# A chain of its own for the queries of an attention layer, and the softmax's division on another engine

## Chip, cores and metric

The kernel runs on one core of one Trainium2 chip. The metric is the device time of one execution in microseconds, as the median of several runs. TensorE (PE in the rows) multiplies matrices, VectorE (DVE) and ScalarE (ACT) work on rows of 128 partitions, GpSimd (POOL) and SyncE (SP) issue most of the DMAs. Each engine works through its own queue in order, and an instruction waits at the head of its queue until its inputs are there and its output's buffer is free.

## What is computed

A two-layer decoder over 528 positions (16 learned ones and 512 of the input), width 1024. Each layer is half a SwiGLU, a mixer, and half a SwiGLU. The mixer of layer 0 is a recurrent one (RWKV-7), which the change does not touch. The mixer of layer 1 is an attention over selected keys; this is what matters here:

```python
q, k, v, qi, ki, wi = jnp.split(h @ w_in, ATT_SPLITS, axis=-1)
q = partial_rope(rms_norm(q.reshape(B, T, 16, 64), q_g), cos, sin)
k = partial_rope(rms_norm(k.reshape(B, T, 4, 64), k_g), cos, sin)
# an indexer scores all keys for each query; the 128 best causal ones count
logits = jnp.einsum("bqgrd,bqkgd->bqgrk", qg, kg).astype(jnp.float32) * scale
logits = jnp.where(valid[:, :, None, None, :], logits, -jnp.inf)
p = jax.nn.softmax(logits, axis=-1).astype(v.dtype)
o = jnp.einsum("bqgrk,bqkgd->bqgrd", p, vg)
```

There are 16 query heads in 4 groups of 4; a group shares one key and one value head.

## The kernel before

Matrix products that need float32 accuracy are made of three faster ones: each operand is split into a rounded part (`_hi`) and the rest (`_lo`). Weights stream from DRAM in units of 1024 columns (`wraw`), ScalarE rounds them (`whi`), VectorE takes the rest (`wlo`).

The positions are worked in two ranges, A (16 to 272) and B (272 to 528). The program has main streams, one after another: feed-forward halves (`ffn`), projections (`idx`, `kvq`), the attention's output projection (`ao`). They use PSUM banks `acc`. Beside them run chains: generators that issue a piece of work and yield what the next piece needs. `run` (L726) takes the main stream piece by piece and, by a list of prices (`Clock`), puts in a piece of a chain when its inputs should be there by the time TensorE gets to it, or when the main stream would have to wait. Chains are held back when VectorE or ScalarE would fall too far behind TensorE (`full`: 1500 ns for the stages kvqA and f10b, 3000 by default and for f11a). `drain` (L747) issues all that is left of the chains, with no main stream beside it. So the order on each engine is fixed when the program is built.

The attention of range A is laid beside the streams kvqA and f10b (the feed-forward half of the other range) and must be over before `ao` of range A; a `drain` stands there. Range B is laid beside kvqB and f11a, with a `drain` before `ao` of range B.

`attend(i, XO)` (L1621) does 128 queries, i from 1 to 4; `Wd` = 16 + 128 i keys, so 144, 272, 400 and 528. A range is two of them (`attend_range`, L1734): 1 and 2, then 3 and 4. Its parts, by heads or groups:

- `turn_q(g)` (L1630): the queries of a group are copied twice side by side (`qsd`, ScalarE), turned by TensorE (4 transposes into a bank `bg`), scaled and rounded into `qs` (ScalarE), and the rest is taken (VectorE). `qs` has 2 buffers, `qsd` 1. The helper is `stacked`.
- `logits(c)` (L1633), a step c of 0 to 7 with two heads: the score matmuls (`bg<-kT,qs`; 4, or 8 in two halves for 528 keys), on VectorE a custom instruction that adds the selection's bias and takes the row minimum (`pr<-bg,bias`, `mn`), on ScalarE the exponential with its row sum (`pr<-pr,mn`, `sm`).
- `divide(hh)` (L1659): the sum's reciprocal and the product, both on VectorE.
- `turn(hh)` (L1664): the probabilities are transposed by TensorE (`bg<-ident,pr`) and copied to `pt` by ScalarE. `pr` has 4 buffers.
- `values(g)` (L1678): the products with V for a group (`ry<-pt,V`); after an odd group ScalarE and VectorE split the result into `xa_hi`, `xa_lo` (or `xb_`).

There are 3 banks `bg` for all chains and one bank `ry`. The loop in `attend` goes over c from 0 to 8: `values` of the group that is complete, `logits(c)`, `turn_q` of the next group after an odd c, and then `divide` and `turn` of the heads of step c - 1.

Of the kernel before, what the change touches and what calls it, by code (L numbers as in the profile page):

```python
# [13 lines left out]
AF = mybir.ActivationFunctionType  # L14
OP = mybir.AluOpType
# [11 lines left out]
QA = (16, 272)  # L27
QB = (272, 528)
# [11 lines left out]
QG, OKA = 152, 154  # L40
# [393 lines left out]
def trunk(ctx, tc, wall, units, h0, vec, cstd, gqk, out, stop=None, gap=0.0, share=400.0, slack=200.0, fulls={}):  # L434
    clock = Clock()
    nc = Core(tc.nc, clock)
# [50 lines left out]
    def col(c):  # L487
        return vecs[:, c:c + 1]
# [4 lines left out]
    def bbank(tag="bg"):  # L493
        return psum.tile([128, 512], F32, name=tag, bufs={"bg": 3, "ry": 1}[tag])
# [213 lines left out]
    def beside(*gens):  # L708
        chains.extend(Chain(g) for g in gens)
        return chains[-len(gens)]  # L710
# [712 lines left out]
    kT = at.tile([128, 4, T], F32R, name="kT")  # L1423
# [6 lines left out]
    qx = {}  # L1430
    have = set()
# [84 lines left out]
    def segments(Wd):  # L1516
        return [(0, Wd)] if Wd <= 512 else [(0, Wd // 2), (Wd // 2, Wd)]
# [103 lines left out]
    def attend(i, XO):  # L1621


        Wd = 16 + 128 * i
        nb = i + 1
        b = bias[i - 1]
        sm = at.tile([128, 16], F32, name="sm", bufs=1)
        pr, pt, po, qs = {}, {}, {}, {}

        def turn_q(g):  # L1630
            qs[g] = yield from stacked("qs", 2, qx[i, g // 2][:, 256 * (g % 2):256 * (g % 2) + 256], col(QG))

        def logits(c):  # L1633

            g = c // 2
            mn = {}
            for o in (0, 1):
                pr[2 * c + o] = at.tile([128, T], F32, name="pr", bufs=4)
                mn[o] = at.tile([128, 2], F32, name="mn", bufs=4)
            sg = segments(Wd)  # L1640
            for j, (s0, s1) in enumerate(sg):
                yield "bg", qs[g], kT[:, g, s0:s1]
                ps = [bbank()[:, :s1 - s0] for _ in range(2)]
                for o in (0, 1):
                    for k in (0, 1):
                        nc.tensor.matmul(ps[o], qs[g][:, k, 2 * (c % 2) + o], kT[:, g, s0:s1],
                                         start=k == 0, stop=k == 1)
                for o in (0, 1):
                    nc.vector.tensor_tensor_reduce(out=pr[2 * c + o][:, s0:s1], in0=ps[o], in1=b[:, s0:s1],
                                                   scale=1.0, scalar=3e38, op0=OP.add, op1=OP.min,  # L1650
                                                   accum_out=mn[o][:, j:j + 1])
            for o in (0, 1):
                lg = pr[2 * c + o]
                if len(sg) == 2:
                    nc.vector.tensor_tensor(mn[o][:, 0:1], mn[o][:, 0:1], mn[o][:, 1:2], op=OP.min)
                nc.scalar.activation(lg[:, :Wd], lg[:, :Wd], AF.Exp, bias=mn[o][:, 0:1], scale=-1.0,
                                     accum_out=sm[:, 2 * c + o:2 * c + o + 1])

        def divide(hh):  # L1659
            r = sm[:, hh:hh + 1]  # L1660
            nc.vector.reciprocal(r, r)
            nc.vector.tensor_scalar(pr[hh][:, :Wd], pr[hh][:, :Wd], r, None, op0=OP.mult)

        def turn(hh):  # L1664
            if hh % 4 == 0:
                pt[hh // 4] = at.tile([128, 5, 4, 128], F32, name="pt", bufs=1)
            to = pt[hh // 4][:, :, hh % 2 * 2 + hh % 4 // 2]
            for k0 in range(0, nb, 4):
                ks = range(k0, min(k0 + 4, nb))
                yield "bg", pr[hh][:, :Wd]  # L1670
                p = bbank()
                pv = p.rearrange("p (m t) -> p m t", t=128)
                for kb in ks:
                    t0 = TOK[kb][0]
                    nc.tensor.transpose(pv[:, kb - k0], pr[hh][:, t0:t0 + 128], ident)
                nc.scalar.activation(to[:, k0:k0 + len(ks)], pv[:, :len(ks)], AF.Copy)

        def values(g):  # L1678

            q, c0 = g // 2, 256 * (g % 2)  # L1680
            yield "ry" if g % 2 == 0 else po[q][:, c0:c0 + 256], pt[g]
            if g % 2 == 0:
                po[q] = bbank("ry")
            for kb in range(nb):
                for o in (0, 1):
                    nc.tensor.matmul(po[q][64 * o:64 * o + 64, c0:c0 + 256], V[:, kb, 64 * g:64 * g + 64],
                                     pt[g][:, kb, 2 * o:2 * o + 2].rearrange("p h t -> p (h t)"),
                                     start=kb == 0, stop=kb == nb - 1)
            if g % 2:
                pv = po[q].rearrange("p (m t) -> p m t", t=128)  # L1690
                s = slice(TOK[i][0] - XO.t0, TOK[i][1] - XO.t0)
                hi, lo = XO.hi[:, 4 * q:4 * q + 4, s], XO.lo[:, 4 * q:4 * q + 4, s]
                nc.scalar.activation(hi, pv, AF.Copy)
                nc.vector.tensor_sub(lo, pv, hi.bitcast(F32))

        yield from turn_q(0)
        for c in range(9):
            if c % 2 and c > 1:
                yield from values(c // 2 - 1)
            if c < 8:  # L1700
                yield from logits(c)
            if c in (1, 3, 5):
                yield from turn_q((c + 1) // 2)
            if c:
                for hh in (2 * c - 2, 2 * c - 1):
                    divide(hh)
                for hh in (2 * c - 2, 2 * c - 1):
                    yield from turn(hh)
        yield from values(3)
        yield 0  # L1710
# [13 lines left out]
    def chain(*gs):  # L1724
        for g in gs:
            yield from g
# [4 lines left out]

    XO = {}

    def attend_range(q, i, name):  # L1734
        while ("q", i + 1) not in have or i - 1 not in bias:
            yield None
        XO[q] = Split(xq, DT, q, name)
        yield from attend(i, XO[q])
        while i not in bias:
            yield None  # L1740
        yield from attend(i + 1, XO[q])
# [3 lines left out]
    def heads_chain():  # L1745

        for _ in range(3):
            while not hs:
                yield None
            yield from hs[0]  # L1750
            hs.pop(0)
# [5 lines left out]
    QI = tiles_of((1, 2, 0), "xb_hi")  # L1757
    run(early(idx(XS["xa"], QI, (0, 1, 2)), norms[3], B))
    beside(heads_chain(), chain(*(idx_heads(i, QI) for i in (0, 1, 2)), select(0), select(1)))
    beside(attend_range(QA, 1, "xa"))  # L1760
    run(early(kvq(XS["xa"], (0, 1, 2)), norms[3], B, X=x_of(B, "xb"), start=40), "kvqA")
    have.add(QA)
    run(ffn(1, 0, B, XS["xb"], hid_of(B), norms[4]), "f10b")
# [2 lines left out]
    QI = tiles_of((3, 4), "xa_hi")  # L1766
    run(early(idx(XS["xb"], QI, (3, 4)), norms[5], QA))
    beside(heads_chain(), chain(idx_heads(3, QI), idx_heads(4, QI), select(2), select(3)))
    beside(attend_range(QB, 3, "xb"))
    run(early(kvq(XS["xb"], (3, 4)), norms[5], QA, X=x_of(QA, "xa"), start=40), "kvqB")  # L1770
    have.add(QB)
    run(ffn(1, 1, QA, XS["xa"], hid_of(QA), None, done=write), "f11a")
# [63 lines left out]
```

## Time and profile before

| | us |
|---|---|
| median of 3 timed runs | 2361.96 (2358.84 to 2363.72) |
| the profiled run | 2355.84 |
| its span in the trace | 2354.1 |
| TensorE busy | 2264.1 |
| VectorE busy | 1704.5 |
| ScalarE busy | 1263.8 |

A span is shorter than the run's time by what lies before the first and behind the last instruction. A busy share is a mean over stages with different limits, so it is read by stretches; the attention of range A starts near 1608 and that of range B near 1955 us from the span's start. In the rows a matmul's duration includes a tail that the next one overlaps; PEclk is TensorE's granted clock, 1.00 for the upper level (2.4 GHz) and 0.50 for the lower.

### The profile page before, as it was taken

To read this page: it belongs to the slowest core of one execution; us is meant where nothing else is said; L and a number is where in the kernel's file an instruction comes from. 1 tells how busy PE (TensorE), PEld (TensorE's weight loads), DVE (VectorE), ACT (ScalarE), POOL (GpSimd) and SP (SyncE) were. 2 spreads that over 40 slices of the span, in tenths; PEclk is the share of its full clock that TensorE was granted. 3 is DMA by queue.
4 is the path that set the end of the run, shared out by engine and by line. 5 is a ranking of instruction groups with operands and counts; after the bars stand their busy time and mean duration, and the time that the engine had idled before them with its cause. 6 is when DMAs were issued, how large, how long until landed. Compare 5 with 4: busy or idle time off the path is not lost.

```text
span 2354.1 us, 49396 instructions
## 1 busy us (share of the span) xinstructions
PE 2264.1 (96%) x20106; PEld 2177.3 (92%) x20106; DVE 1704.5 (72%) x3283; ACT 1263.8 (54%) x2135; POOL 175.5 (7%) x226
## 2 busy tenths in 40 slices
PE   8998899999989999999999999999988999999999
PEld 8998889999889999999999999899977899988999
DVE  7667888856897975677566565689755898766665
ACT  5443665465548535655444444556664646775543
POOL 0001521010043111000000000000000000000000
PEclk9999999999999999999999999999989999999999
DMA  6553334632434444245554555455532453434554
GB/s 231 180 172 123 119 126 162 205 86 83 144 118 157 156 161 147 74 135 171 174 178 171 180 187 177 148 171 174 167 117 79 147 179 129 159 117 135 185 183 144
DMA packets 101555, 355.98 MB, mean 151 GB/s; under 512 B 11552, under 2 KB 15728, under 8 KB 101328
## 3 DMA queue, kind: packets, MB, share of 16 engines
q1 hardware_dynamic: 99120, 347.91, 44.5%
q0 software_dynamic: 2208, 4.92, 0.8%
q8 instruction: 158, 2.59, 0.4%
q14 instruction: 69, 0.57, 0.1%
HBM read 348.51 MB, written 4.28 MB: 150 GB/s over the span
## 4 chain that ended last, share of the span: by engine, by line
PE 79%; DVE 13%; ACT 4%; issue 2%; DMA 1%; POOL 1%; SPq 0%; DVEq 0%; ACTq 0%; POOLq 0%
PE acc L341 68%; PE bg L341 8%; DVE wlo L341 4%; PE ry L341 4%; DVE tb L341 2%; ACT whi L341 1%; DVE pr L341 1%; DMA wraw<-wall 1%; ACT pr L341 1%; DVE ynat L341 0%; DVE h L341 0%; DVE st L341 0%; DVE m L341 0%; DVE bu L341 0%; DVE rel L341 0%
## 5 line engine op out<-in xcount | busy, mean ns | idle before, releaser
L341 DVE TENSOR_TENSOR wlo<-wraw,whi 128x1024 fp32r<-128x1024 f32 (+1 forms) x658 | 810.4, 1235 | 167.4 <-ACT whi L341 166.6
L341 ACT ACTIVATE whi<-wraw 128x1024 fp32r<-128x1024 f32 (+1 forms) x658 | 688.3, 1051 | 437.6 <-PE acc L341 265.8
L341 PE MATMUL acc<-hid_hi,whi 128*128 128x256 f32 (+1 forms) x1408 | 407.4, 289 | 3.4 <-DVE h L341 2.2
L341 PE MATMUL acc<-hid_lo,whi 128*128 128x256 f32 (+1 forms) x1408 | 399.1, 283 | 0.8 <-DVE hid_lo L341 0.8
L341 PE MATMUL acc<-hid_hi,wlo 128*128 128x256 f32 (+1 forms) x1408 | 399.4, 284 | 0.0
L341 PE MATMUL acc<-xa_hi,whi 128*128 128x256 f32 (+1 forms) x1088 | 311.4, 286 | 1.9 <-ACT xa_hi L341 1.9
L341 PE MATMUL acc<-xa_lo,whi 128*128 128x256 f32 (+1 forms) x1088 | 309.0, 284 | 2.4 <-DVE xa_lo L341 2.3
L341 PE MATMUL acc<-x_hi,whi 128*128 128x272 f32 (+1 forms) x1024 | 302.8, 296 | 8.2 <-ACT whi L341 6.1
L341 PE MATMUL acc<-xa_hi,wlo 128*128 128x256 f32 (+1 forms) x1088 | 309.4, 284 | 0.5 <-DVE wlo L341 0.4
L341 PE MATMUL acc<-x_hi,wlo 128*128 128x272 f32 (+1 forms) x1024 | 294.5, 288 | 0.2 <-DVE wlo L341 0.2
L341 PE MATMUL acc<-x_lo,whi 128*128 128x272 f32 (+1 forms) x1024 | 294.2, 287 | 0.0
L341 PEld LDWEIGHTS acc<-hid_hi,whi 128*128 128x128 f32 x1408 | 264.9, 188 | 8.3 <-issue 4.0
L341 PEld LDWEIGHTS acc<-hid_lo,whi 128*128 128x128 f32 x1408 | 266.3, 189 | 1.0 <-DVE hid_lo L341 1.0
L341 PEld LDWEIGHTS acc<-hid_hi,wlo 128*128 128x128 f32 x1408 | 265.2, 188 | 0.2 <-DVE wlo L341 0.2
L341 PE MATMUL acc<-xb_hi,whi 128*128 128x256 f32 x752 | 213.6, 284 | 0.0
L341 PE MATMUL acc<-xb_hi,wlo 128*128 128x256 f32 x752 | 211.6, 281 | 0.0
L341 PE MATMUL acc<-xb_lo,whi 128*128 128x256 f32 x752 | 211.6, 281 | 0.0
L341 PEld LDWEIGHTS acc<-xa_hi,whi 128*128 128x128 f32 x1088 | 206.3, 190 | 3.3 <-ACT xa_hi L341 2.1
L341 PEld LDWEIGHTS acc<-xa_lo,whi 128*128 128x128 f32 x1088 | 206.5, 190 | 2.9 <-DVE xa_lo L341 2.9
L341 PEld LDWEIGHTS acc<-x_hi,whi 128*128 128x128 f32 x1024 | 195.2, 191 | 13.9 <-ACT whi L341 6.1
L341 PEld LDWEIGHTS acc<-xa_hi,wlo 128*128 128x128 f32 x1088 | 206.3, 190 | 0.9 <-DVE wlo L341 0.9
L341 PEld LDWEIGHTS acc<-x_hi,wlo 128*128 128x128 f32 x1024 | 194.9, 190 | 0.9 <-DVE wlo L341 0.9
(317 smaller groups left out, 4393.0 us busy)
## 6 DMA issues: line engine op xcount, KB each, us to landing
wraw<-wall SPq DMA_DIRECT2D x644, 512.0 KB, 3.4
wraw<-wall SPq DMA_DIRECT2D x10, 438.0 KB, 3.3
out<-h SPq DMA_DIRECT2D x8, 256.0 KB, 2.3
h<-h SPq DMA_DIRECT2D x2, 512.0 KB, 8.1
ynat<-L POOLq DMA_DIRECT2D x2, 512.0 KB, 5.0
T<-ynat POOLq DMA_DIRECT2D x2, 512.0 KB, 4.1
gm<-T POOLq DMA_DIRECT2D x4, 224.0 KB, 6.4
wraw<-wall SPq DMA_DIRECT2D x2, 402.0 KB, 2.9
```

What stands on the lines that cost most here:

```text
L341: r = f(*args, **kw)
```

## The change

`turn_q` leaves `attend` and becomes a chain of its own for each range, with the 8 groups of its two `attend`s in order. It may turn group k when the scores of group k - 2 have been issued (its `qs` buffer is then free as soon as they are done). `logits` waits, while the program is built, until its group's queries have been issued. The product of `divide` goes from VectorE to ScalarE, in place, with the reciprocal as the factor; the reciprocal stays on VectorE.

```diff
-        pr, pt, po, qs = {}, {}, {}, {}
-
-        def turn_q(g):
-            qs[g] = yield from stacked("qs", 2, qx[i, g // 2][:, 256 * (g % 2):256 * (g % 2) + 256], col(QG))
+        pr, pt, po = {}, {}, {}
 
         def logits(c):
 
             g = c // 2
+            while (i, g) not in qs:
+                yield None
+            q = qs[i, g]
...
         def divide(hh):
             r = sm[:, hh:hh + 1]
             nc.vector.reciprocal(r, r)
-            nc.vector.tensor_scalar(pr[hh][:, :Wd], pr[hh][:, :Wd], r, None, op0=OP.mult)
+            nc.scalar.activation(pr[hh][:, :Wd], pr[hh][:, :Wd], AF.Copy, scale=r)
...
-        yield from turn_q(0)
         for c in range(9):
             if c % 2 and c > 1:
                 yield from values(c // 2 - 1)
             if c < 8:
                 yield from logits(c)
-            if c in (1, 3, 5):
-                yield from turn_q((c + 1) // 2)
+            if c < 8 and c % 2:
+                have.add(("logits", i, c // 2))
...
+    qs = {}
+
+    def turn_q(i):
+
+        groups = [(j, g) for j in (i, i + 1) for g in range(4)]
+        for k, (j, g) in enumerate(groups):
+            while ("q", j) not in have or (k > 1 and ("logits", *groups[k - 2]) not in have):
+                yield None
+            qs[j, g] = yield from stacked("qs", 2, qx[j, g // 2][:, 256 * (g % 2):256 * (g % 2) + 256], col(QG))
...
-    beside(attend_range(QA, 1, "xa"))
+    beside(attend_range(QA, 1, "xa"), turn_q(1))
...
-    beside(attend_range(QB, 3, "xb"))
+    beside(attend_range(QB, 3, "xb"), turn_q(3))
```

The order on TensorE behind the last matmul of f10b (the first row of each fence), where `drain` lays the end of `attend(2)`. `pr` rows are transposes of one head, `kT,qs` rows the scores of a head, `qsd` a query turn, `ry` a `values`. Before:

```order
L341 MATMUL acc_21960<-hid_hi_19158,wlo_21850 128x256
L341 MATMUL bg_21986<-ident_85,pr_21661 128x128 x3
L341 MATMUL bg_21991<-ident_85,pr_21663 128x128 x3
L341 MATMUL ry_21996<-pt_21839,V_18527 64x256 x6
L341 MATMUL bg_22007<-kT_18525,qs_21832 128x272 x2
L341 MATMUL bg_22008<-kT_18525,qs_21832 128x272 x2
L341 MATMUL bg_22019<-ident_85,qsd_22017 128x128 x4
L341 MATMUL bg_22032<-ident_85,pr_21882 128x128 x3
L341 MATMUL bg_22037<-ident_85,pr_21884 128x128 x3
L341 MATMUL bg_22046<-kT_18525,qs_22024 128x272 x2
L341 MATMUL bg_22047<-kT_18525,qs_22024 128x272 x2
L341 MATMUL bg_22060<-ident_85,pr_22003 128x128 x3
```

and after:

```order
L341 MATMUL acc_22022<-hid_hi_19158,wlo_21880 128x256
L341 MATMUL bg_22062<-ident_85,qsd_21971 128x128 x4
L341 MATMUL bg_22070<-ident_85,pr_21933 128x128 x3
L341 MATMUL bg_22075<-ident_85,pr_21935 128x128 x3
L341 MATMUL ry_21926<-pt_21961,V_18527 64x256 x6
L341 MATMUL bg_22092<-kT_18525,qs_21907 128x272 x2
L341 MATMUL bg_22093<-kT_18525,qs_21907 128x272 x2
L341 MATMUL bg_22107<-ident_85,pr_22015 128x128 x3
L341 MATMUL bg_22112<-ident_85,pr_22017 128x128 x3
L341 MATMUL bg_22121<-kT_18525,qs_22067 128x272 x2
L341 MATMUL bg_22122<-kT_18525,qs_22067 128x272 x2
L341 MATMUL bg_22135<-ident_85,pr_22088 128x128 x3
```

Before, the scores in this piece are those of steps 3 and 4, with the query turn of group 2 between them; after, they are those of steps 5 and 6, and the one query turn, of group 3, stands first. Steps 3 and 4 now lie beside f10b.

The order on ScalarE in the drain of range B, from the exponentials of step 6 of `attend(4)` (rows with `sm` on the left are exponentials, `pt` rows copies of transposed probabilities). Before:

```order
L341 ACTIVATE pr_26225,sm_25461<-pr_26225,mn_26226 128x528
L341 ACTIVATE pr_26227,sm_25461<-pr_26227,mn_26228 128x528
L341 ACTIVATE pt_26197<-bg_26253 128x4x128
L341 ACTIVATE pt_26197<-bg_26259 128x128
L341 ACTIVATE pt_26197<-bg_26262 128x4x128
L341 ACTIVATE pt_26197<-bg_26268 128x128
L341 ACTIVATE pr_26282,sm_25461<-pr_26282,mn_26283 128x528
L341 ACTIVATE pr_26284,sm_25461<-pr_26284,mn_26285 128x528
```

and after:

```order
L341 ACTIVATE pr_26225,sm_25549<-pr_26225,mn_26226 128x528
L341 ACTIVATE pr_26227,sm_25549<-pr_26227,mn_26228 128x528
L341 ACTIVATE pr_26155<-pr_26155,sm_25549 128x528
L341 ACTIVATE pr_26157<-pr_26157,sm_25549 128x528
L341 ACTIVATE pt_26194<-bg_26207 128x4x128
L341 ACTIVATE pt_26194<-bg_26213 128x128
L341 ACTIVATE pt_26194<-bg_26216 128x4x128
L341 ACTIVATE pt_26194<-bg_26222 128x128
L341 ACTIVATE pr_26282,sm_25549<-pr_26282,mn_26283 128x528
L341 ACTIVATE pr_26284,sm_25549<-pr_26284,mn_26285 128x528
L341 ACTIVATE pr_26225<-pr_26225,sm_25549 128x528
L341 ACTIVATE pr_26227<-pr_26227,sm_25549 128x528
```

The divides of the heads of step 5 now stand behind the exponentials of step 6, ahead of their own copies. On TensorE the drain of range B holds the same rows before and after.

## Rows read from the trace of the kernel before

**Rows 1.** The page's first part: busy time, share, instructions of each engine.

```profile
PE 2264.1 (96%) x20106; PEld 2177.3 (92%) x20106; DVE 1704.5 (72%) x3283; ACT 1263.8 (54%) x2135; POOL 175.5 (7%) x226
```

**Rows 2.** By stretches: length, busy of PE, PEld, DVE, ACT, POOL, clock, DMA, GB/s.

```profile
1725.00:1748.10 23.10, 23.03 (x191) 22.59 (x190) 17.16 (x43) 18.20 (x36) 0.00 (x0) 1.00 0.45 149
1748.10:1786.80 38.70, 24.32 (x121) 16.98 (x119) 14.23 (x53) 16.24 (x42) 0.00 (x0) 0.74 0.05 21
...
2100.00:2119.50 19.50, 17.11 (x138) 15.04 (x136) 12.92 (x38) 12.85 (x25) 0.00 (x0) 1.00 0.38 124
2119.50:2138.80 19.30, 14.64 (x99) 10.02 (x97) 9.43 (x39) 8.79 (x25) 0.00 (x0) 1.00 0.12 41
```

**Rows 3.** Timeline, TensorE, end of range A: start, length, instructions, [idle before <-releaser].

```profile
1748.10 0.82 PE L341 MATMUL bg<-ident,pr 128*128 128x128 f32 x6
...
1753.53 1.27 PE L341 MATMUL bg<-kT,qs 128*128 128x272 f32 x4
...
1760.90 1.25 PE L341 MATMUL bg<-kT,qs 128*128 128x272 f32 x4
...
1767.19 0.77 PE L341 MATMUL bg<-kT,qs 128*128 128x272 f32 x4
...
1774.58 1.25 PE L341 MATMUL bg<-kT,qs 128*128 128x272 f32 x4
...
1780.86 0.77 PE L341 MATMUL bg<-kT,qs 128*128 128x272 f32 x4
...
1786.79 0.39 PE L341 MATMUL acc<-xa_hi,whi 128*128 128x256 f32 x1
```

**Rows 4.** Timeline, the same drain, step 5 of attend(2) from its exponentials' end.

```profile
1770.04 0.61 ACT L341 ACTIVATE qsd<-q 128x512 f32<-128x512 f32 x1
...
1771.40 0.69 ACT L341 ACTIVATE qs<-bg,vecs 128x512 fp32r<-128x512 f32 x1 [0.75 <-PE bg L341]
1772.12 0.75 DVE L341 SCALAR_TENSOR_TENSOR qs<-bg,vecs,qs 128x512 fp32r<-128x512 f32 x1 [2.78 <-ACT qs L341]
...
1773.39 1.54 PE L341 MATMUL bg<-ident,pr 128*128 128x128 f32 x6 [2.03 <-DVE pr L341]
```

**Rows 5.** Timeline, all engines, end of range B, steps 6 and 7 of attend(4).

```profile
2122.66 1.55 PE L341 MATMUL bg<-kT,qs 128*128 128x264 f32 x8
...
2124.95 0.73 ACT L341 ACTIVATE pr<-pr,mn 128x528 f32<-128x528 f32 x1 [1.68 <-DVE mn L341]
...
2125.15 0.49 DVE L341 TENSOR_SCALAR pr<-pr,sm 128x528 f32<-128x528 f32 x1
...
2125.70 1.67 PE L341 MATMUL bg<-ident,pr 128*128 128x128 f32 x10 [1.48 <-DVE pr L341]
...
2126.40 1.41 ACT L341 ACTIVATE pt<-bg 128x512 f32<-128x512 f32 x4
...
2130.00 1.56 PE L341 MATMUL bg<-kT,qs 128*128 128x264 f32 x8
...
2132.90 3.24 PE L341 MATMUL bg<-ident,pr 128*128 128x128 f32 x20 [1.35 <-DVE pr L341]
...
2136.07 2.77 PE L341 MATMUL ry<-pt,V 128*64 128x256 f32 x20
2138.78 0.39 PE L341 MATMUL acc<-xb_hi,whi 128*128 128x256 f32 x1
```

**Rows 6.** Groups by shape: count | busy us, mean ns of one | idle before them.

```profile
L341 ACT ACT_TABLE_LOAD x40 | 51.3, 1283 | 4.4 <-DMA h<-h 3.8
...
L341 ACT ACTIVATE tb<-h 128x256 f32<-128x256 f32 x42 | 16.6, 412 | 23.8 <-DVE h L341 23.8
...
L341 ACT ACTIVATE qsd<-q 128x512 f32<-128x512 f32 x16 | 9.9, 616 | 0.0
...
L341 DVE TENSOR_SCALAR pr<-pr,sm 128x528 f32<-128x528 f32 x16 | 7.9, 496 | 0.6
...
L341 DVE TENSOR_SCALAR pr<-pr,sm 128x272 f32<-128x272 f32 x16 | 5.8, 362 | 0.6
```

More of the change, by code (lines that the diff above doesn't have):

```diff
@@ L1641, in logits @@
             for j, (s0, s1) in enumerate(sg):
-                yield "bg", qs[g], kT[:, g, s0:s1]
+                yield "bg", q, kT[:, g, s0:s1]
                 ps = [bbank()[:, :s1 - s0] for _ in range(2)]
@@ L1645, in logits @@
                     for k in (0, 1):
-                        nc.tensor.matmul(ps[o], qs[g][:, k, 2 * (c % 2) + o], kT[:, g, s0:s1],
+                        nc.tensor.matmul(ps[o], q[:, k, 2 * (c % 2) + o], kT[:, g, s0:s1],
                                          start=k == 0, stop=k == 1)
```

## Prediction

> **What bounds the kernel now.** I read the page first: TensorE is busy for 2264.1 of 2354.1 us [rows 1], so a change off TensorE can pay only where TensorE stands still or runs slow. The table by stretches shows where that is in the part that the change touches [rows 2]. Beside the feed-forward matmuls TensorE loses nothing: in the 23.1 us before 1748.1 it is busy for 23.03, in 191 matmuls, one every 0.12 us. Then the main stream of stage f10b ends and `drain()` lays the rest of the attention down alone. I call that drain A: 1748.1 to 1786.8, 38.7 us, TensorE's granted clock 0.74 on average, so about half of it at the lower level (1.2 GHz). The same thing after f11a is drain B: 2119.5 to 2138.8, 19.3 us, at full clock, 14.64 us of it busy. Just ahead of drain B TensorE is idle for 2.4 of 19.5 us.
>
> The timeline of TensorE in drain A gives its rhythm [rows 3]. The first score matmul (kT, qs) of step 3 starts 5.4 us after the main stream's end; from there on the steps are 7.4, 6.3, 7.4 and 6.3 us long, and the last, with its two turns, 5.9. The sum is the 38.7. The odd steps 3 and 5 are 1.1 us longer, though step 5 ran its score matmuls at full clock (0.77 us against 1.27 for four); these are the steps that turn queries. [rows 4] show why: after the exponentials ScalarE copies the queries (1770.04), TensorE turns them, ScalarE scales (1771.40), VectorE splits (1772.12), and only behind that stand VectorE's divides, so the transposes of `pr` come at 1773.39, 3.35 us after the exponentials' end.
>
> **The change part by part.**
>
> *What drain A loses.* By the order, five score steps (3 to 7) and two query turns lay behind the main stream; now there are three score steps (5 to 7) and one query turn, which stands right at the start, where TensorE waits anyhow for ScalarE's last squares and copies. I go step by step. The start: again about 5.5 us to the score matmuls (5.4 before). Step 5 without the query turn: the divide can follow the exponentials at once; on ScalarE it costs 0.43 us, worked out below, so the transposes come 0.48 us behind the exponentials in place of 3.35: 7.4 - 2.9 gives 4.5. Step 6: 6.3 + 0.5 = 6.8, since the divides now stand behind both exponentials on ScalarE, where VectorE did them beside the second. Step 7 and the end: 5.9 + 0.5 + 0.9 = 7.3, the 0.9 for the divides of heads 14 and 15, which now queue on ScalarE behind two copies of `pt`. Sum 24.1, so drain A is 14.6 us shorter. By the clock this may be 22 (all of it at the upper level) to 26 us.
>
> *What that costs in the main stream.* The work taken out of drain A goes beside f10b, where TensorE has no room. It is one query turn (4 matmuls), two score steps (8), two pairs of heads turned (12) and one values group (12 in the trace): 36 matmuls. At 0.12 us each that is 4.3 us; taken by the durations of the drain's rows, tails included, it would be near 6. Net gain of A: 14.6 - 4.3 = 10.3 us.
>
> *The divide on ScalarE, its price.* VectorE's TENSOR_SCALAR takes 0.362 us for 272 columns and 0.496 for 528 [rows 6]. A copy from SBUF on ScalarE is not shown for these widths; the nearest rows are `qsd` with 512 columns, 0.616 us, and the square of `h` with 256, 0.412. The slope is 0.80 ns a column, so 0.425 for 272 and 0.63 for 528. One divide is thus a sixth to a quarter dearer; what counts is whose queue it stands in.
>
> *Drain B gets longer.* Its content on TensorE is the same before and after, row for row; there is no query turn in it either way. So only the divide tells. In step 6 [rows 5] the score matmuls start at 2122.66, the first exponential at 2124.95; VectorE divides the pair before it at 2125.15, beside that exponential, and the transposes start at 2125.70, 3.04 us after the score matmuls. ScalarE's two exponentials end at 2126.40, 3.74 us after them, and there its copies of `pt` begin. Now the divides come behind the exponentials: the first ends at 3.74 + 0.63, the transposes start at about 4.4: 1.3 us later, and the copies, the values and step 7 with them. Step 7 (2130.00, transposes at 2132.90, end at 2138.78) has this again (1.3), and at its end the divides of heads 14 and 15 stand behind four copies: before they lay on VectorE while ScalarE copied; now two of them, some 1.0 us, lie in the chain ahead of the last values at 2136.07. At the drain's start the score step 5 now stands only 9 main matmuls ahead of its end, so its exponentials and the divide are not covered: from 3.2 us (2119.5 to 2122.66) to about 4.0, 0.8. Sum: 0.8 + 1.3 + 1.3 + 1.0 = 4.4 us longer. The floor is 2.5 (step 7's divides hidden by the waits for free banks), the ceiling 7.
>
> *ScalarE ahead of the drains.* In the 23.1 us before drain A ScalarE is busy for 18.2 [rows 2]. About eight divides (2.9), two pairs of exponentials (some 2.1) and four copies (1.4) come in; the stretch grows by 4.3. That makes 24.6 in 27.4 us, 90%, and in a queue that runs in order a divide waits behind exponentials whose scores aren't there yet. The room it takes from VectorE is worth nothing there: TensorE did not wait. Ahead of drain B it is 12.85 + 8 x 0.53 = 17.1 in 19.5 us, where TensorE already idles 2.4. I take 1 us of new waits in each, 2 in all; the bounds are 0 and 6.
>
> *Tables.* ScalarE's order from the attention on has 36 table loads in place of 30. A load takes 1.283 us and ScalarE was idle for 4.4 us ahead of all 40 of the kernel [rows 6], so six cost 7.7 us of ScalarE, spread over some 310 us; that is inside the 2 us above. The Trainium skill (ScalarE: Activation LUTs, What ACT_TABLE_LOAD costs) gives 2.66 us for a switch, a drain included. By that rule six would cost 16 us of ScalarE. The trace doesn't agree, as idle time of 0.11 us a load leaves no room for the drain; had the rule been right, the slower rival below would gain weight.
>
> *Clock.* Drain B kept full clock at 14.64 busy in 19.3 us, 76%. With 4.4 us more it is 62%, near drain A, which fell (24.32 of 38.7, 63%, part of that at the lower level). If it falls in the last step, its 20 transposes and the values cost about 3 us more; I take 1, a third of it.
>
> *Else.* The 16 query turns and 64 divides keep their number, no DMA is added or moved on its queue, and the reciprocals stay on VectorE. The two query turns made early for attend(3) lie beside f11a's matmuls as they did before.
>
> **Sum.** -14.6 + 4.3 + 4.4 + 2 + 1 = -2.9 us. The profiled run of 2355.84 us becomes 2352.9. The three timed runs have a median of 2361.96, 6.1 us above the profiled one, so I forecast on that scale: 2359.1 us.
>
> **The rivals.**
>
> *Faster, 2352 us.* Drain A stays at the upper clock level and takes 22 us (gain 16.7), new waits are nil since the planner puts the divides where there is room, drain B loses only 2.5: -16.7 + 4.3 + 2.5 = -9.9. For it: the shorter drain has less time at low density, and VectorE, free of 64 divides, reaches the score step sooner. Against it: drain A's clock was already down at its second step.
>
> *Slower, 2368 us.* ScalarE becomes the engine that paces the end of both stages. Place: the divides behind the exponentials in ScalarE's queue, ahead of TensorE's transposes. Price: 6 us of waits ahead of the drains, drain B longer by 7 with its clock fallen (3), drain A 26 us (gain 12.7): -12.7 + 4.3 + 7 + 3 + 6 = +7.6, that is 2369.6; with half of those waits 2366.6; I say 2368. It decides from the point where ScalarE's work between two score steps exceeds TensorE's: at 90% ahead of drain A it is not far.
>
> *Nothing is won.* The drain is as long as before, since the steps that left it were covered by something else. Then the 4.3 us moved would not be a cost either, and drain B's loss alone would stand: 2366. The steps' lengths in [rows 3] speak against it: they add up to the whole drain.
>
> **How the numbers follow.** A change that a measurement of this kernel can tell from none is about 0.2%, 4.7 us. The likeliest case lies within it, at -2.9, with a chance of 0.47; its own range is 2357.3 to 2366.7. Faster by more than 4.7 us: 0.35, nearly all of it the first rival and cases between it and the forecast. Slower by more: 0.18, the second rival and the worse half of the third. The range goes from the faster rival to near the slower one, 2352 to 2367, and leaves about one in ten out on each side.
>
> **What would show it.** In the profile after: the stretch between the last f10b matmul and the first of `ao` near 24 us (38.7 before), with three score steps in it; the same stretch after f11a near 24 (19.3). In drain B transposes 4.4 us behind the score matmuls of a step, with ScalarE's divides right ahead of them. TensorE's waits for `pr` put down to ScalarE where they were VectorE's. The forecast is wrong if drain A stays above 30 us, if drain B is no longer than 20, or if TensorE's new waits ahead of the two drains come to more than 6 us.

## The result, and the profile after

The changed kernel takes 2379.2 us in the median of its runs (2378.4 to 2380.4), against 2361.5 for the kernel before: a ratio of 1.0076, with an interval of 1.0058 to 1.0093. It is 17.7 us slower, where 2359.1 had been forecast and 2367 was the end of the range. The profiled run has a span of 2376.6 us, 22.5 more than before.

The page's busy times, engine by engine, to be held against [rows 1]:

```profile
PE 2276.8 (96%) x20106; PEld 2189.9 (92%) x20106; DVE 1679.1 (71%) x3219; ACT 1298.4 (55%) x2205; POOL 174.4 (7%) x226
```

TensorE has the same 20106 matmuls and is busy for 12.7 us longer, which goes with its clock (0.978 over the whole run, 0.985 before); ScalarE has 34.6 us more, 64 products and six table loads. The stretches are those of [rows 2], from the last matmul of f10b to `ao` (drain A), from the last of f11a (drain B), each with the stretch ahead of it, and last the rest of the program:

```profile
1730.00:1761.50 31.50, 28.73 (x226) 27.50 (x226) 18.98 (x45) 26.84 (x55) 0.00 (x0) 0.95 0.36 123
1761.50:1791.60 30.10, 20.35 (x85) 13.84 (x84) 6.68 (x31) 15.34 (x42) 0.00 (x0) 0.62 0.06 18
2100.00:2130.90 30.90, 26.65 (x204) 24.24 (x200) 16.45 (x53) 20.09 (x35) 0.00 (x0) 0.94 0.38 123
2130.90:2159.10 28.20, 19.30 (x97) 14.60 (x97) 4.59 (x28) 15.24 (x36) 0.00 (x0) 0.70 0.03 10
2159.10:2376.60 217.50, 213.35 (x1789) 213.14 (x1788) 139.42 (x228) 98.29 (x134) 0.00 (x0) 1.00 0.53 170
```

Drain A did get shorter, 30.1 us for 38.7. But the main stream ahead of it ends 13.4 us later than before, drain B takes 28.2 for 19.3, and in the stretches ahead of the drains TensorE is idle for 2.8 of 31.5 us, where it lost almost nothing before, and for 4.3 of 30.9, at a granted clock of 0.95 and 0.94. Over the whole main streams beside the attention (the first two rows are before, the others after) its idle time grew from 0.3 to 6.3 us and from 13.9 to 19.1:

```profile
1600.00:1748.10 148.10, 147.79 (x1238) 144.46 (x1237) 113.16 (x269) 101.56 (x181) 0.00 (x0) 1.00 0.48 160
1786.80:2119.50 332.70, 318.81 (x2435) 299.69 (x2434) 269.37 (x606) 203.49 (x344) 0.00 (x0) 0.99 0.44 144
1600.00:1761.50 161.50, 155.19 (x1267) 150.18 (x1266) 110.63 (x258) 116.87 (x217) 0.00 (x0) 0.98 0.45 147
1791.60:2130.90 339.30, 320.21 (x2434) 301.80 (x2434) 260.08 (x586) 217.22 (x367) 0.00 (x0) 0.98 0.44 143
```

TensorE's waits over the attention (waited for, total us, times, longest) name VectorE's probabilities before (first row, 1600 to 2160 us), and now ScalarE's and their copies (1600 to 2180 us):

```profile
PE bg L341 <- DVE pr L341: 8.3, 5, 2.0
...
PE bg L341 <- ACT pr L341: 16.5, 9, 2.9
PE bg L341 <- ACT pt L341: 9.2, 4, 4.1
```

The timeline of drain B shows one step, as [rows 5] did. The score matmuls start at 2134.27, the exponentials wait for VectorE's minimum, the two products stand behind them, and TensorE's transposes wait for the first of these:

```profile
2132.70 1.88 PE L341 MATMUL bg<-ident,pr 128*128 128x128 f32 x10 [1.82 <-ACT pr L341]
...
2134.27 2.26 PE L341 MATMUL bg<-kT,qs 128*128 128x264 f32 x8
...
2137.17 0.73 ACT L341 ACTIVATE pr<-pr,mn 128x528 f32<-128x528 f32 x1 [2.28 <-DVE mn L341]
...
2137.90 0.72 ACT L341 ACTIVATE pr<-pr,mn 128x528 f32<-128x528 f32 x1
...
2138.62 1.34 ACT L341 ACTIVATE pr<-pr,sm 128x528 f32<-128x528 f32 x2
...
2139.39 2.39 PE L341 MATMUL bg<-ident,pr 128*128 128x128 f32 x10 [2.87 <-ACT pr L341]
...
2141.72 3.77 PE L341 MATMUL ry<-pt,V 128*64 128x256 f32 x20
...
2145.42 0.99 PE L341 MATMUL bg<-kT,qs 128*128 128x264 f32 x6
```

The step is 11.15 us long (2134.27 to 2145.42); before it was 7.34 [rows 5]. The transposes come 5.1 us behind the score matmuls (3.04 before), after a wait of 2.87 us, and TensorE runs at a lower clock. It had fallen to 0.50 already for the score matmuls, behind the wait of 1.82 us at 2132.70, and is 0.61 for the transposes and the values: eight score matmuls take 2.26 us (1.55 before), ten transposes 2.39 (1.67), the values 3.77 (2.77).

One more thing is new. ScalarE's rows a little ahead of drain B:

```profile
2102.97 1.28 ACT L341 ACT_TABLE_LOAD   x1 [3.62 <-DVE mn L341]
2104.26 0.74 ACT L341 ACTIVATE pr<-pr,mn 128x528 f32<-128x528 f32 x1
```

The table load for the exponentials waited 3.62 us for VectorE's minimum, though it needs no data, and only then loaded for 1.28. The groups of ScalarE show the same as a sum (count, busy us, mean ns, idle us ahead):

```profile
L341 ACT ACT_TABLE_LOAD x46 | 59.0, 1283 | 19.5 <-DVE mn L341 14.8 <-DMA h<-h 4.0
...
L341 ACT ACTIVATE pr<-pr,sm 128x528 f32<-128x528 f32 x16 | 10.8, 722 | 0.0
...
L341 ACT ACTIVATE pr<-pr,sm 128x272 f32<-128x272 f32 x16 | 7.4, 508 | 0.0
```

Ahead of the table loads ScalarE idled for 4.4 us before [rows 6] and now for 19.5, of which 14.8 for that minimum. The program's list of instructions tells why. In the changed kernel an exponential can have two waits, one for VectorE's minimum and one for ScalarE's own earlier product in the same buffer; then the load ahead of it carries one of the two. Nine loads of this part carry the wait on VectorE, and eight of them make up the 14.8 us; before, none did.

### The profile page after: what moved, and what is told of

Its sections match the earlier page's. It is cut to its first block, busy times and chain, and to the rows that moved or that the text cites. A ratio compares the mean times of both kernels' runs of the same rounds, so it can differ in the third digit from the quotient of the medians.

```text
span 2376.6 us, 49445 instructions
## 1 busy us (share of the span) xinstructions
PE 2276.8 (96%) x20106; PEld 2189.9 (92%) x20106; DVE 1679.1 (71%) x3219; ACT 1298.4 (55%) x2205; POOL 174.4 (7%) x226
## 4 chain that ended last, share of the span: by engine, by line
PE 78%; DVE 13%; ACT 5%; issue 2%; DMA 1%; POOL 0%; SPq 0%; DVEq 0%; ACTq 0%; POOLq 0%
PE acc L341 67%; PE bg L341 8%; DVE wlo L341 4%; PE ry L341 3%; DVE tb L341 2%; ACT whi L341 2%; ACT pr L341 1%; DMA wraw<-wall 1%; DVE ynat L341 1%; DVE st L341 0%; DVE pr L341 0%; DVE bu L341 0%; ACT L341 0%; DVE rel L341 0%; DVE m L341 0%
```

## The experiments

In the diffs, `tc.nc` issues an instruction of which the planner isn't told, and `clock.add` tells the planner of one that isn't issued there. With the two together TensorE's order stays the same, instruction for instruction, while another engine's work is changed. The medians of the kernel before lay between 2359.7 and 2361.5 us from one set of runs to the next, so differences between sets are good to about 2 us. Where a drain begins and ends is read from each trace's timeline: the start of the last matmul of the main stream plus 0.12 us, to the first of `ao`.

### Each part alone

The chain alone is the changed kernel with this edit:

```diff
-            nc.scalar.activation(pr[hh][:, :Wd], pr[hh][:, :Wd], AF.Copy, scale=r)
+            nc.vector.tensor_scalar(pr[hh][:, :Wd], pr[hh][:, :Wd], r, None, op0=OP.mult)
```

> The query chain as in the changed kernel, the product of the divide back on VectorE. Four theories for the 17.7 us. Q (queue order: the divides stand behind the next exponentials in ScalarE's queue, and TensorE's transposes wait for them): faster than before, 2345 to 2353 us, since drain A keeps its three steps at 24 to 27 us and TensorE's waits for pr put down to ScalarE (16.5 us from 1500 us to the end in the changed kernel) are gone. B (the early query turns hold banks and the work moved beside f10b costs more than 4.3 us): 2368 us or more, with the wait of 3.4 us near 1642 still there. L (ScalarE has too much to do, wherever the divides stand): as Q, 2345 to 2355. T (table loads that carry the exponential's wait on VectorE): none of the loads carries it here, so as Q.

Measured: 2340.0 us, a ratio of 0.9914 (0.9899 to 0.9929). The chain by itself gains 20 us, more than any of the theories had said. Its two drains, in the table by stretches:

```profile
1753.20:1775.80 22.60, 15.39 (x84) 10.06 (x82) 10.43 (x37) 10.35 (x29) 0.00 (x0) 0.85 0.07 24
2117.50:2121.70 4.20, 4.06 (x32) 2.71 (x30) 0.76 (x3) 1.55 (x5) 0.00 (x0) 1.00 0.73 236
```

Drain A takes 22.6 us, and of drain B only 4.2 are left, since its score steps now lie beside f11a. B, the theory that the early query turns cost the time, is out: the chain is good. The opposite part is the kernel before with the product on ScalarE, the same edit the other way round:

> The kernel before with the product of the divide on ScalarE, the query turns where they were. Q: slower than before by 10 to 18 us, 2372 to 2380, drain A 40 to 43 us (38.7 before) and drain B near 28 (19.3), TensorE's waits for pr put down to ScalarE. L: the same, 2372 to 2380. B: 2361 to 2366, since the chain is not there. T: 8 of its table loads carry a wait on VectorE, 8 x 1.28 = 10 us at most, 2366 to 2372.

Measured: 2387.5 us, 1.0117 (1.0101 to 1.0132), even slower than expected. TensorE's waits for `pr` put down to ScalarE came to 25.7 us, and drain B to 46.1, because the planner laid more of range B behind f11a (152 matmuls for 96); drain A kept 38.1. So the whole loss comes with the product. What it is about the product, the other runs have to tell.

### Order or engine

The planner prices the product as ScalarE's work and lays another order. Two runs take the order from one engine's prices and make the product on the other:

```diff
 # order of the changed kernel, product on VectorE
-            nc.scalar.activation(pr[hh][:, :Wd], pr[hh][:, :Wd], AF.Copy, scale=r)
+            p = pr[hh][:, :Wd]
+            tc.nc.vector.tensor_scalar(p, p, r, None, op0=OP.mult)
+            clock.add("scalar", "activation", (p, p, AF.Copy), dict(scale=r))
 # order of the chain alone, product on ScalarE
-            nc.scalar.activation(pr[hh][:, :Wd], pr[hh][:, :Wd], AF.Copy, scale=r)
+            p = pr[hh][:, :Wd]
+            tc.nc.scalar.activation(p, p, AF.Copy, scale=r)
+            clock.add("vector", "tensor_scalar", (p, p, r, None), dict(op0=OP.mult))
```

> The changed kernel, whose planner still prices the product as ScalarE's, with the product itself on VectorE: TensorE's order is that of the changed kernel, instruction for instruction. It splits the 39 us between the changed kernel (2379.2) and the chain alone (2340.0) in two. E (the engine: the product's place and time in ScalarE's queue cost it): 2345 to 2356, drain A 23 to 26 us and drain B, whose rows are those of the kernel before, 19 to 21. O (the order that the planner lays by ScalarE's prices costs it): 2365 to 2380. No table load should carry a wait on VectorE.

> The other half: the order of the chain alone, laid by VectorE's prices, with the product on ScalarE. E: the engine alone costs 20 to 30 us here too, 2360 to 2370, with 6 table loads that carry a wait on VectorE and TensorE's waits for pr and pt put down to ScalarE. O: 2340 to 2350, since the order is the good one.

Measured: 2350.9 (0.9961, 0.9946 to 0.9976) and 2369.3 (1.0037, 1.0024 to 1.0050).

| | product on VectorE | product on ScalarE | difference |
|---|---|---|---|
| order laid by VectorE's prices | 2340.0 | 2369.3 | 29.3 |
| order laid by ScalarE's prices | 2350.9 | 2379.2 | 28.3 |
| difference | 10.9 | 9.9 | |

The engine costs 28 to 29 us in either order, the order another 10 to 11. With the product on VectorE the changed kernel's drains are these, with the same TensorE rows as in the changed kernel:

```profile
1757.00:1780.90 23.90, 16.72 (x84) 10.89 (x82) 10.57 (x43) 11.31 (x31) 0.00 (x0) 0.79 0.06 23
2115.40:2133.50 18.10, 14.53 (x98) 9.98 (x96) 8.51 (x37) 9.84 (x28) 0.00 (x0) 1.00 0.04 15
```

Held against the changed kernel's stretches this splits the 27.8 us between the two spans. In the drains TensorE is busy 3.6 (A) and 4.8 us (B) longer for the same matmuls, at a clock of 0.62 and 0.70 in place of 0.79 and 1.00; it is idle 2.6 and 5.3 longer; and the two main streams take 4.7 longer each, nearly all of it idle time (from 1600 us on 8.7 us more, by the same table). So 8.4 of the 27.8 are matmuls at a lower clock. The other 2.2 lie behind drain B and can't be put down to the product: TensorE's rows there are the same in all runs, and the traces take 215.3 to 217.5 us for them, 216.7 with the chain alone and 215.3 with the changed kernel and the early table loads below. Ahead of the attention, too, traces of the same rows differ, by up to 3 us: the last matmul ahead of the first query turn starts at 1599.11 in the changed kernel and at 1601.08 here. Counted from there, the first main stream is 6.6 us longer, not 4.7.

### Moved ahead, the planner laying the order

The divides are issued ahead of the next step's scores, once with the product on ScalarE and once with it on VectorE; the planner lays a new order for each:

```diff
+            if c:
+                for hh in (2 * c - 2, 2 * c - 1):
+                    divide(hh)
             if c < 8:
                 yield from logits(c)
...
             if c:
-                for hh in (2 * c - 2, 2 * c - 1):
-                    divide(hh)
```

> The changed kernel with the divides of step c - 1 issued ahead of the scores of step c, so that on ScalarE they stand ahead of step c's exponentials. The same number of instructions on every engine but for two table loads fewer. Q: at least 20 us faster than the changed kernel, 2345 to 2357, TensorE's waits for pr put down to ScalarE below 5 us in all (16.5 in the changed kernel). L: 2370 to 2380, as ScalarE has the same work. B: 2368 or more. T: only 1 load carries a wait on VectorE, against 9; 8 x 1.28 = 10 us, 2369.

> The chain alone (product on VectorE) with the divides of step c - 1 issued ahead of the scores of step c, the order of program that gained 19 us where the product was ScalarE's. E and O: on VectorE the divides never stood behind the exponentials, so there is little to gain: 2335 to 2345 (2340.0 without). Against the same program with the product on ScalarE (2360.0) it tells what ScalarE costs where its divides stand ahead of the exponentials: E, some 20 us, mostly waits for scores and banks ahead of the drains; O, drains of the same length in both and no more than 5 us.

Measured: 2360.0 with ScalarE's product (0.9999, 0.9989 to 1.0009) and 2340.3 with VectorE's (0.9917, 0.9903 to 0.9932). With the product on ScalarE the move gains 19 us, on VectorE nothing. TensorE's waits for `pr` fell to 3.4 us, as the queue theory said, but the time came out worse than that theory's 2357: both drains are short (24.5 and 0 us), and the main stream ahead of drain B is longer, 361.6 us from `ao` of range A to the end of f11a, against 332.7 before. As the order changed with it, this pair doesn't split place from load.

### The table loads

A one-column exponential of a constant ahead of a step's last score matmuls has the table loaded there; the planner doesn't see it:

```diff
+    nc.vector.memset(small[:, 2:4], 0.0)
...
+    warm = at.tile([128, 1], F32, name="warm")
...
+                if j == len(sg) - 1 and clock.table != AF.Exp:
+                    tc.nc.scalar.activation(warm, small[:, 2:3], AF.Exp)
```

> The changed kernel with a one-column exponential of a constant on ScalarE ahead of a step's last score matmuls, in the 18 steps whose exponentials need a table load; the planner's prices don't see it, so TensorE's order is the same instruction for instruction, and the same 46 loads are there, but none of them now carries a wait on VectorE (9 did). T: 8 to 11.5 us faster than the changed kernel, 2368 to 2371 (nine loads of 1.28 us that now lie in the wait for VectorE). Q, L and B: 2376 to 2380, since the waits that count are those for the divides or the banks.

> The chain alone with the one-column exponential ahead of the scores, as in the run that gained 8 us on the changed kernel. None of its 42 table loads carries a wait on VectorE without it, so if that wait was the reason, nothing is gained here: 2338 to 2342 (2340.0 without). If the earlier place of the load in itself was the reason, it gains here too: 2332 to 2336.

Measured: 2370.9 on the changed kernel (1.0042, 1.0027 to 1.0057), 8.3 us less than without; 2338.8 on the chain alone (0.9909, 0.9893 to 0.9926), 1.2 us less, inside the spread. So the gain goes with the loads that carried the wait, not with the early place. Nine loads of 1.28 us would be 11.5. The trace of the changed kernel with the early loads, near the place shown above:

```profile
2094.72 1.28 ACT L1646 ACT_TABLE_LOAD   x1
2096.01 0.20 ACT L1646 ACTIVATE warm<-small 128x1 f32<-128x1 f32 x1
...
2098.34 0.74 ACT L341 ACTIVATE pr<-pr,mn 128x528 f32<-128x528 f32 x1 [2.13 <-DVE mn L341]
```

The load is over 2.3 us before the exponential starts, and costs nothing there.

### The place in the queue, in a fixed order

These runs keep the changed kernel's order on TensorE and the product on ScalarE. First the products alone were moved, ahead of the next exponentials; the reciprocals stayed on VectorE where they were, behind the next step's bias instructions (this stands in `logits`, between those and the loop with the exponentials; the products of the last step, which no scores follow, stay where they were here and below):

```diff
+            if c:
+                for hh in (2 * c - 2, 2 * c - 1):
+                    product(hh, tc.nc)
             for o in (0, 1):
...
```

> The changed kernel with one thing moved: on ScalarE the products of step c - 1 stand ahead of the exponentials of step c, not behind them. TensorE's order is that of the changed kernel, instruction for instruction, and the same products are made on ScalarE. With the product on VectorE this order took 2350.9, with it on ScalarE 2379.2, so 28.3 us are to be explained. P (the place behind the exponentials): 15 to 25 us of them go, 2354 to 2364, drain A near 25 and drain B near 20; as 8 of the 9 table loads that carried the wait on VectorE no longer do, the 8.3 us measured for these are in that. W (the time that the products take on ScalarE): only the table loads' share goes, 2369 to 2372.

> The run with the products ahead of the exponentials, plus the one-column exponential ahead of the scores that gained 8.3 us on the changed kernel. P and W: one table load alone still carried the wait on VectorE there, so at most 1.3 us are gained. If the early place of the load is worth something in itself, 4 to 8 us are gained.

Measured: 2389.0 (1.0120, 1.0105 to 1.0135), 10 us slower where 15 to 25 faster were expected; and with the early table loads 2376.4 (1.0061, 1.0044 to 1.0078), 12.6 us less, where 1.3 at most were expected. Both misses have one reason, in ScalarE's rows:

```profile
2116.89 1.37 ACT L1668 ACTIVATE pr<-pr,sm 128x528 f32<-128x528 f32 x2 [3.82 <-DVE sm L1667]
2118.27 1.28 ACT L341 ACT_TABLE_LOAD   x1
2119.57 0.74 ACT L341 ACTIVATE pr<-pr,mn 128x528 f32<-128x528 f32 x1
```

The product waited 3.82 us for its reciprocal, which stood on VectorE behind the next scores' bias instructions; over the run ScalarE waited so 27 times, for 70.6 us. So the wait for the next scores was still at the head of ScalarE's queue, and behind it came products, table load and exponentials, one after another. In 15 places a table load stands right behind such a product; with the early load it is ahead of the wait. It isn't the place relative to the exponentials that counts, but what stands behind the wait for the next scores.

Then reciprocals and products both were issued ahead of the next step's scores, with nothing else changed:

```diff
         def logits(c):
...
+            if c:
+                for hh in (2 * c - 2, 2 * c - 1):
+                    product(hh, tc.nc)
             mn = {}
...
+        def divide(hh):
+            if hh > 13:
+                return product(hh, nc)
...
+            clock.add("vector", "reciprocal", (r, r), {})
+            clock.add("scalar", "activation", (p, p, AF.Copy), dict(scale=r))
```

> The changed kernel, TensorE's order the same instruction for instruction, with the reciprocals and products of step c - 1 issued ahead of the scores of step c: on VectorE the reciprocals stand ahead of step c's bias instructions, on ScalarE the products ahead of its exponentials. The run before that put the products there but left the reciprocals behind the bias instructions lost 10 us. P (the place counts, if the product need not wait for a reciprocal that stands behind the next step's scores): 2360 to 2368, that is the table loads' 8 us (one of 46 carries the wait on VectorE here) and up to 9.5 more. W (only the time that the products take on ScalarE, and the table loads, count): 2370 to 2372. N (any place ahead of the exponentials delays these and costs more than it saves): 2376 or more.

Measured: 2354.2 us (0.9977, 0.9968 to 0.9987), 25 us less than the changed kernel, more than expected, and 3.3 above the same order with VectorE's product. The same products, on the same engine, with TensorE in the same order. Drain B, in the timeline and as a stretch:

```profile
2117.87 1.56 PE L341 MATMUL bg<-kT,qs 128*128 128x264 f32 x8
2118.35 1.36 ACT L1665 ACTIVATE pr<-pr,sm 128x528 f32<-128x528 f32 x2
...
2119.49 1.33 PE L341 MATMUL bg<-ident,pr 128*128 128x128 f32 x9
...
2120.15 0.73 ACT L341 ACTIVATE pr<-pr,mn 128x528 f32<-128x528 f32 x1 [0.44 <-DVE mn L341]
...
2125.18 1.56 PE L341 MATMUL bg<-kT,qs 128*128 128x264 f32 x8
```

```profile
2115.20:2136.30 21.10, 15.68 (x98) 11.27 (x96) 5.00 (x28) 14.22 (x35) 0.00 (x0) 0.92 0.04 14
```

The products run while TensorE does the next scores and VectorE the bias; ScalarE would have been idle then (for 1.68 us ahead of the exponential in [rows 5]). The transposes follow the score matmuls at once, 1.6 us after their start in place of 5.1, and the step is 7.31 us long. The main streams are short again as well: f10b ends at 1758.7 us, and from `ao` of range A to f11a's end it takes 332.5, together 9.6 us less than in the changed kernel. This run moves the reciprocals on VectorE too, but these alone can't be the gain: in the changed kernel no wait of ScalarE's ended on a reciprocal.

### How long the product takes

Here the product is made for the first 16 columns alone and the rest of a row is left undivided:

```diff
-            nc.scalar.activation(pr[hh][:, :Wd], pr[hh][:, :Wd], AF.Copy, scale=r)
+            p = pr[hh][:, :Wd]
+            tc.nc.scalar.activation(p[:, :16], p[:, :16], AF.Copy, scale=r)
+            clock.add("scalar", "activation", (p, p, AF.Copy), dict(scale=r))
```

> The changed kernel with the product on ScalarE made for the first 16 columns alone (the rest of each row is left undivided, so this part of the computation is left out), at the same place in the queue and with the same waits; orders and table loads are those of the changed kernel. W (duration): a product of 272 columns takes 0.46 us and one of 528 0.67 there, of which some 0.25 remain, so the two of a step save 0.4 to 0.85 us; over the five steps of the drains that is 3.5 us and beside the main streams about as much, 2370 to 2373. P (place): 2374 to 2379.

> The changed kernel with the product for 16 columns alone (the rest is left undivided, so that part is left out) and the one-column exponential ahead of the scores. Apart they gained 10.5 and 8.3 us. If they are two causes, they add up: 2379.2 - 18.8 = 2360, and some 9 us are left to the place behind the exponentials and to the two instructions' fixed cost. If both only shorten one and the same wait, 2364 to 2369.

> As the run with reciprocals and products ahead of the scores, and the products for 16 columns alone (the rest is left out). Place, duration and table loads are all taken away, while two instructions a step stay on ScalarE. P and W together: 2350 to 2356, what the same order takes with the product on VectorE (2350.9). If something else is in the 28.3 us, 2360 or more.

Measured: behind the exponentials 2368.7 (1.0035, 1.0022 to 1.0048), 10.5 us less than with the whole row and somewhat more than the 6 to 9 expected; with the early loads as well 2362.3 (1.0009, 1.0000 to 1.0019); ahead of the scores 2352.0 (0.9963, 0.9951 to 0.9975), 2.2 us less than with the whole row there. So the product's length costs 10.5 us behind the wait and 2.2 ahead of it, within the spread. Length and table loads together gain 16.9 of 18.8: nearly two separate terms, both of them work behind the same wait. Taken together with the place, 27 of the 28.3 us are accounted for.

### The same move in the other order

> The order of the chain alone (laid by VectorE's prices), with the product on ScalarE and with reciprocals and products issued ahead of the next step's scores. In that order the product took 2340.0 on VectorE and 2369.3 on ScalarE behind the exponentials. P (the place is the cause, here too): 25 to 27 of these 29.3 us are won back, 2342 to 2345; the order and the place are then two separate losses. If the place pays only in the order of the changed kernel: 2355 or more. Faster than 2340 would mean that VectorE's relief is worth something.

Measured: 2352.9 us (0.9964, 0.9952 to 0.9977). Only 16.4 of the 29.3 us came back here, so the expectation failed: the place pays in this order too, but 13 us are left. In the changed kernel's order 3 were left. The main streams hold most of the rest: compared with the chain alone, drain A is 2.3 us longer and drain B 0.9, but f10b ends 5.8 later, and `ao` of range A to f11a's end is 348.1 us in place of 341.7. That order lays more steps beside f11a; whether it is there the products' length or their reciprocals' place on VectorE was not tried.

## Why the prediction was wrong

By the stretches, the 22.5 us of the span are -8.8 in drain A, 13.4 and 6.6 in the main streams ahead of the drains, 9.0 in drain B and 2.2 behind it. Point by point, in the order of the prediction's sum:

- **Drain A, -14.6.** Right for the chain, wrong for the change. With the product on VectorE the changed kernel's order gives 23.9 us, where 24.1 stood in the sum; with it on ScalarE 29.9. The step that failed is the pricing of its parts: the start took 7.5 us (5.5 was said), step 5 took 4.65 (4.5), step 6 7.9 (6.8), step 7 with the end 9.9 (7.3). They are read from these rows, from one start of score matmuls to the next, the main stream having ended at 1761.56:

```profile
1769.06 1.27 PE L341 MATMUL bg<-kT,qs 128*128 128x272 f32 x4
1772.52 1.54 PE L341 MATMUL bg<-ident,pr 128*128 128x128 f32 x6 [2.18 <-ACT pr L341]
1773.71 1.26 PE L341 MATMUL bg<-kT,qs 128*128 128x272 f32 x4
...
1781.60 1.03 PE L341 MATMUL bg<-kT,qs 128*128 128x272 f32 x4
...
1791.46 0.58 PE L341 MATMUL acc<-xa_hi,whi 128*128 128x256 f32 x1
```

- **Moved work, +4.3.** The chain alone has 5.1 there, so for that order the term was sound. In the order that the planner laid for the change it is 8.8 with the product on VectorE, for the same matmuls moved (f10b ends at 1756.9 us, before at 1748.1): 3.7 us of the order's cost, for which the sum had no term, lie here.
- **Drain B, +4.4, ceiling 7.** It was 9.0. The chain of the step was told rightly: transposes 4.4 us behind the score matmuls were forecast, 5.1 came. What failed is the price of the matmuls behind that delay: but for the 1 us under Clock they were priced at full clock, and in the same order they were busy 14.5 us with VectorE's product and 19.3 with ScalarE's.
- **ScalarE ahead of the drains, +2, bounds 0 and 6.** This is the step that failed by most. Against the same order with VectorE's product each main stream is 4.7 us longer, 9.4 in all, and TensorE's idle time there is 8.7 longer; with reciprocals and products ahead of the scores 9.6 us of the main streams are won back. The room on ScalarE was taken as a sum of busy times (24.6 in 27.4 us). But in [rows 5] and in the rows after, ScalarE's queue stands still at the exponential until VectorE's minimum is there, and what counts is how much stands behind it. A share of busy time can't show that.
- **Tables, inside the 2 us.** Six more loads were priced by their length. That nine of them would come to wait for VectorE wasn't seen; it is 8.3 us in the run that undoes it. The rule weighed there, 2.66 us for a switch by the Trainium skill (ScalarE: Activation LUTs, What ACT_TABLE_LOAD costs), is not the reason: all 46 loads still take 1283 ns, and of the 19.5 us of idle time ahead of them 14.8 ended on that minimum and 4.0 on a DMA, which leaves no room for a drain.
- **Clock, +1.** It was meant for drain B's last step alone. Against the same order with VectorE's product the lower clock cost 4.8 us in drain B, and 3.6 in drain A, which are in the terms above.
- **The product's price, 0.425 and 0.63 us.** It was 0.51 and 0.72. The copies that were taken as the nearest rows have no factor by partition, as the product has. The Trainium skill (ScalarE: Activation LUTs, What ACT_TABLE_LOAD costs) gives some 93 ns for each such operand, and the rows agree: 0.72 is 0.09 above the 0.63 estimated.
- **The order.** The sum took the drains' content from the order as it was laid, and that was right. It didn't ask what the order itself had cost: laid by VectorE's prices, the chain would have left 4.2 us of drain B. On either engine the order laid by ScalarE's prices costs 10 to 11 us; which of its rows cost them was not taken apart further.

The slower rival named the right place, "the divides behind the exponentials in ScalarE's queue, ahead of TensorE's transposes", and got the size wrong: +7.6, where +17.7 came. Its condition was wrong too. It was to decide from where "ScalarE's work between two score steps exceeds TensorE's"; with the products ahead of the scores ScalarE has the same work, and the same order loses 3 us.

Of the signs that the prediction had set for itself, those of the mechanism came: ScalarE's products stand right ahead of the transposes, and TensorE's waits for `pr` are put down to ScalarE. Those of the size came out against it: drain A ended at the limit of 30 us and not near 24, drain B at 28, and TensorE's idle time in the two main streams grew by 11.2 us (14.2 to 25.4), where 6 was the limit.

## What to carry to other kernels

Before work is put on an engine with room, find the wait at which its queue stands still, and ask on which side of that wait the work will come: this kernel's 64 products cost 28 us behind the wait for the next scores and 3 ahead of it (29 and 13 in the denser order). What the moved work itself waits for, even a small instruction on another engine, has to be issued ahead of that wait as well; moving the product without its reciprocal cost 10 us more. And a change with two parts is two forecasts: here one part gained 20 us and the other lost 39, and the kernel with the first part alone, at 2340.0 us, is faster than both.

## What the runs showed of the hardware

- A table load can stand in the queue for a semaphore of the exponential behind it, though it needs none of its data (with the early exponential the loads were over before the minimum was there). Nine loads carried such a wait, and 14.8 us of ScalarE's idle time ended on it. A one-column exponential ahead of the wait, at 0.20 us, moved the load out and gained 8.3.
- The same TensorE rows were busy for 14.5 us at a granted clock of 1.00 and for 19.3 at 0.70. TensorE's waits were up to 2.9 us long in the slow stretch and up to 1.5 in the other. So in these two drains the added waits cost about twice what they lasted: 5.3 us more of idle time came with 4.8 of slower matmuls in drain B, and 2.6 with 3.6 in drain A.
